# Output projections of the long sequence as seven products of halves, summed in PSUM

## The chip, the core and the metric

The kernel runs on one core of one Trainium2 chip. The metric is the device time of one execution in microseconds (us); lower is better. The core has five engines that work side by side, each with its own queue: PE (TensorE, matrix products; its weight loads, PEld, run beside them), DVE (VectorE), ACT (ScalarE), POOL (GpSimd) and SP (SyncE), which here issues nearly all DMAs. SBUF is the memory on the chip, PSUM the small memory that PE writes its sums to, DRAM the large one outside.

## The reference

Two batches share their weights: x_prompt with 512 positions (below Q, the short sequence) and x_sample with 1024 (S, the long one), 1024 channels each, in float32. There are two layers and a last norm:

```python
# even layer
p = rms_norm(x, g_norm) @ w_in                  # 1024 -> 2560
a = conv31(a_val * sigmoid(a_glu)) + conv_b     # depthwise, 512 channels
a = silu(layer_norm(a)) * silu(a_z)
f = einsum(real(fft2(f_in per group)), w_four) * silu(f_z)
x = x + concat([a, f]) @ w_out                  # 1024 -> 1024
# odd layer
u, bg, cg, z = split(rms_norm(x, g_norm) @ w_in, 4)   # 1024 -> 4096
v = conv3(cg * u) + conv_b                      # depthwise
x = x + (bg * v * silu(z)) @ w_out              # 1024 -> 1024
# at the end
y = rms_norm(x, final_norm)
```

## The kernel before, in words

Channels lie on the 128 partitions and positions along the free dimension. A tile is 128 channels x 512 positions, 8 tiles make the channels, S has two chunks of 512 positions and Q has one. A weight comes in tiles of 128 output channels with all 1024 input channels, 512 KB each.

**Precision.** A float32 matmul is done as three matmuls of a rounded type, float32r. `split` makes the high part `hi` by an ACT copy and the low part `lo = x - hi` on DVE or POOL; then high x high, high x low and low x high are added up in PSUM (`project`, L174). A projection of one tile of outputs is 3 x 8 = 24 matmuls of 512 columns. `load_w` (L133 to L135) loads and splits a weight tile, the low part on POOL.

**Products of halves.** In layer 2's input projection of S (`l2_in_two`) two tiles of output channels (128 x 2) and two chunks of positions (512 x 2) are done at once. With the input channels cut in two halves this is a 2 x 2 matrix of blocks times another, done with seven block products instead of eight (Strassen's scheme in Winograd's form). A product is 4 tiles of input channels x 3 = 12 matmuls. `halves` loads the four blocks of the left side (weights), makes the four sums s1 to s4 of them on DVE and splits the seven operands; `prep_acts_a`, `prep_acts_b` and `prep_far` make the seven right operands (activations) with their sums, two of them by way of DRAM for lack of room. `project_two` runs the seven products, each in a PSUM bank of its own (L673), and adds the results up in SBUF: one ACT copy (L677) and seven DVE adds. Both output projections (`l1_out`, and `l2_out` with `l2_out_last`) use plain projections, chunk by chunk.

**Normalization.** `SqSum` adds up squares per position over the tiles as they come (ACT square, DVE add). `rstd_bcast` sums over partitions with PE, takes the inverse root on DVE with a dozen small instructions, and spreads it with PE.

**Room.** SBUF tiles come from pools by tag with a fixed number of buffers: H 32, F 16, FQ 8, T 8, ap 4, ld 4, lx 2, dp 4. PSUM has four banks for matmul results (tag mm), two for small things (st), two for the wide convolution result (cv). What finds no room goes to DRAM and is loaded again (`ld`).

**Order.** The program text gives a priority. A planner with its own costs of instructions places each instruction on its engine's queue: it takes the ready instruction of the highest priority and may thus mix matmuls of two projections. On the chip each queue then runs in that order, whatever the real times are. The stages around the change, in the text's order: norm of Q's layer 1 result (`norm_mid`), Q's layer 2 input projection (`l2_in`, 8 steps of four projections u, c, z, b) with S's layer norms beside it, S's gates, `l1_out` of S's two chunks, operands of S (`prep_acts_a`), Q's last projection (`l2_out`) with `prep_acts_b` beside it, `prep_far`, eight steps of `l2_in_two`, `l2_out` of S's first chunk, and `l2_out_last` of its second, in two halves of 256 positions so that the end is short. `finish` scales by the last norm and stores.

## Time and profile before

| what | value |
|---|---|
| runs | 1204.4 us median of 3 (1201.76 to 1205.83) |
| profiled execution | 1203.0 us span; it has no other time of its own |
| PE busy | 1150.0 us, 96% |
| DVE, ACT, POOL busy | 77%, 36%, 32% |
| matmuls | 5328 |
| granted PE clock, mean | 0.981 of full speed |
| DMA | 145.45 MB, mean 121 GB/s |

An engine's busy time is the time in which one of its instructions runs. A matmul's row is longer than the distance to the next one's start, since they are pipelined; PE's pace is read from start to start. A group's row gives line, engine, operation, out<-in by the program's names and shapes, count, busy us, mean ns of one, and the engine's idle time before these instructions with what ended it. A timeline row gives start, duration, engine and line.

### The profile page before, as it was taken

The page shows a single profiled execution, that of the slowest core. Times are in us where ns is not written, and L with a number is a line of the kernel's source. Part 1 is how long each engine was busy: PE and PEld are TensorE (multiplying, and loading weights), DVE is VectorE, ACT ScalarE, POOL GpSimd, SP SyncE. Part 2 cuts the span into 40 slices and gives each one's busy share as a digit, 9 for nine tenths or more (in the row PEclk, how much of TensorE's full clock was granted, in tenths as well). Part 3 has the DMA queues.
Part 4 walks back from the last instruction along what each step waited for, and adds up shares of the span by engine and source line. Part 5 has one row for each costly group of instructions (what it writes and reads, how often), then busy time and mean ns, then how long its engine had stood idle before and what let it go on. Part 6 is the DMA issues. An engine that isn't in the chain of part 4 may idle for free.

```text
span 1203.0 us, 14742 instructions
## 1 busy us (share of the span) xinstructions
PE 1150.0 (96%) x5328; PEld 953.4 (79%) x5328; DVE 921.5 (77%) x1414; ACT 427.7 (36%) x673; POOL 387.6 (32%) x205
## 2 busy tenths in 40 slices
PE   7999989999998999999999998989999999999995
PEld 6777858888977887888888886778888888888894
DVE  6899999999998999854235466988877668677465
ACT  6533331224242335532224244542323233234341
POOL 3333432222234454454444433301011110103542
PEclk9999989999998999999999999999999999999997
DMA  9323212101113524232324577843212221124452
GB/s 342 105 72 122 88 36 71 53 36 53 59 65 124 185 93 141 96 123 98 122 100 171 193 262 260 287 143 128 100 54 79 90 71 68 62 96 154 149 196 88
DMA packets 64873, 145.45 MB, mean 121 GB/s; under 512 B 7200, under 2 KB 11552, under 8 KB 64800
## 3 DMA queue, kind: packets, MB, share of 16 engines
q1 hardware_dynamic: 64512, 144.21, 34.9%
q8 instruction: 42, 0.69, 0.2%
q10 hardware_dynamic: 288, 0.30, 0.1%
q14 instruction: 31, 0.25, 0.1%
HBM read 121.93 MB, written 22.54 MB: 120 GB/s over the span
## 4 chain that ended last, share of the span: by engine, by line
PE 75%; DVE 14%; DMA 3%; issue 2%; ACT 1%; SPq 0%; DVEq 0%; ACTq 0%
PE m L673 25%; PE o L174 17%; DVE cv L507 6%; PE c L174 4%; PE b L174 4%; PE z L174 4%; PE u L174 4%; PE az L174 3%; PE glu L174 3%; PE val L174 3%; PE fz L174 2%; PE fb L174 2%; PE fa L174 2%; DVE acc L110 2%; DMA y<-yd 2%
## 5 line engine op out<-in xcount | busy, mean ns | idle before, releaser
L135 POOL TENSOR_TENSOR wl<-wf,wh 128x1024 fp32r<-128x1024 f32 (+1 forms) x134 | 310.7, 2323 | 487.3 <-ACT wh L134 186.6
L134 ACT CAST wh<-wf 128x1024 fp32r<-128x1024 f32 (+1 forms) x134 | 133.1, 998 | 248.6 <-PE o L174 39.5
L507 DVE SCALAR_TENSOR_TENSOR cv<-a,par_sb,cv 128x1024 f32<-128x1024 f32 x120 | 154.2, 1285 | 1.6
L110 POOL TENSOR_TENSOR wo<-wf,wo 128x512 fp32r<-128x512 f32 x32 | 41.3, 1290 | 269.3 <-ACT wo L658 160.4
L673 PE MATMUL m<-bsh,wo 128*128 128x512 f32 x384 | 122.9, 394 | 3.9 <-ACT wo L658 3.9
L110 DVE TENSOR_TENSOR mc<-m,mc 128x512 f32<-128x512 f32 x96 | 64.6, 687 | 67.9 <-PE m L673 67.0
L110 DVE TENSOR_TENSOR acc<-acc,sq 128x512 f32<-128x512 f32 (+1 forms) x79 | 86.1, 1091 | 19.5 <-ACT sq L237 19.2
L507 DVE SCALAR_TENSOR_TENSOR cv<-ap,par_sb,cv 128x512 f32<-128x512 f32 x120 | 90.2, 752 | 2.0
L673 PEld LDWEIGHTS m<-bsh,wo 128*128 128x128 f32 x384 | 72.7, 189 | 20.2 <-ACT wo L658 4.3
L673 PE MATMUL m<-bh,wo 128*128 128x512 f32 x256 | 81.5, 390 | 0.8 <-ACT wo L658 0.8
L673 PE MATMUL m<-bfh,wo 128*128 128x512 f32 x256 | 81.6, 390 | 0.0
L673 PE MATMUL m<-bsl,wo 128*128 128x512 f32 x192 | 76.2, 397 | 0.0
L658 ACT CAST wo<-as 128x512 fp32r<-128x512 f32 x64 | 39.5, 622 | 101.6 <-PE m L673 44.2
L658 ACT CAST wo<-wf 128x512 fp32r<-128x512 f32 x48 | 29.8, 622 | 88.4 <-PE m L673 88.3
L174 PE MATMUL o<-ysh,wh 128*128 128x512 f32 (+1 forms) x256 | 56.2, 343 | 4.4 <-ACT ysh L115 4.3
L673 PEld LDWEIGHTS m<-bh,wo 128*128 128x128 f32 x256 | 48.0, 188 | 11.2 <-ACT wo L658 1.2
L174 PE MATMUL o<-yl,wh 128*128 128x512 f32 x192 | 52.1, 396 | 4.9 <-DVE yl L110 4.9
L673 PEld LDWEIGHTS m<-bfh,wo 128*128 128x128 f32 x256 | 48.1, 188 | 10.2
L174 PE MATMUL o<-ysl,wh 128*128 128x512 f32 (+1 forms) x256 | 55.5, 339 | 0.5 <-DVE ysl L110 0.5
L174 PE MATMUL o<-ysh,wl 128*128 128x512 f32 (+1 forms) x256 | 54.5, 337 | 0.0
L174 PE MATMUL o<-yh,wh 128*128 128x512 f32 x192 | 53.0, 400 | 1.2 <-ACT yh L115 1.2
L174 PE MATMUL o<-yh,wl 128*128 128x512 f32 x192 | 51.7, 392 | 0.0
(316 smaller groups left out, 2440.1 us busy)
## 6 DMA issues: line engine op xcount, KB each, us to landing
wf<-w SPq DMA_DIRECT2D x78, 512.0 KB, 3.5
wf<-w SPq DMA_DIRECT2D x68, 256.0 KB, 2.9
wf<-w1o SPq DMA_DIRECT2D x24, 512.0 KB, 3.5
wf<-w2o SPq DMA_DIRECT2D x16, 512.0 KB, 4.3
x1d<-xr SPq DMA_DIRECT2D x24, 256.0 KB, 2.1
x1r<-x1d SPq DMA_DIRECT2D x24, 256.0 KB, 3.6
y<-yd SPq DMA_DIRECT2D x22, 256.0 KB, 3.7
x<-xs SPq DMA_DIRECT2D x16, 256.0 KB, 5.4
```

Of the source, the lines that this page charges most:

```text
L110: return eng.tensor_tensor(out=out, in0=a, in1=b, op=op)
L134: nc.scalar.copy(wh[i], src_i)
L135: nc.gpsimd.tensor_tensor(out=wl[i], in0=src_i, in1=wh[i].bitcast(F32), op=ALU.subtract)
L174: nc.tensor.matmul(out[:, 0:width], a[k], act[k][b][:, cols], start=(n == 0), stop=(n == 3 * KD - 1))
L507: nc.vector.scalar_tensor_tensor(out=acc, in0=src[:, t:t + n], scalar=col(w0 + t), in1=acc, op0=ALU.mult, op1=ALU.add)
L658: nc.scalar.copy(hi, t)
L673: nc.tensor.matmul(out, w[p][a][:, k * P:(k + 1) * P], ops[p][k][b], start=(n == 0), stop=(n == 11))
```

## The change

`Pair` takes the place of `halves` and `project_two`, and now serves three projections of S: the one into layer 2 as before, and both output projections (`l1_out_two`, `l2_out_two`), in four pairs of output tiles each, for both chunks at once. The order of products is 1, 5, 2, 6, 7, 4, 3. Products 1, 6, 7 and 4 are added up in one PSUM bank (X), 5 and 3 in a second (Z), and 2 has a third (Y). Between the products of a bank its sum so far is read out: `before[..]` and `after[..]` say by what. Signs of operand 4 are changed so that it can be added. `run` makes the weights of a product three products ahead.

The right operands of the output projections are new (`out_ops`, `l2_out_ops`), and `l2_ops` takes the place of `prep_acts_a` and `prep_acts_b`. Weights come in pieces of 256 KB, four buffers of them, also in `load_w`. In the middle stage all low parts of weights are made on POOL. S's a_z and the results of layer 2 go to DRAM and back. Q's normed activations now lie in FQ and F.

The order of stages is now: norm of Q, Q's l2_in for j = 0 to 4 with S's layer norms, gates and the first operands beside them, `l1_out_two`, a second norm of Q, l2_in for j = 5 to 7 with `l2_ops` beside them, the eight steps of layer 2 of S, `l2_out_two`, and Q's output projection in half widths at the end, with S's last scaling and stores beside it.

```diff
+    def wtile():
+        return pool.tile([P, KD * P], F32R, name=nm("wo"), tag="wo", bufs=4)
...
+        t = pool.tile([P, CH], F32, name=nm("wf"), tag="wf", bufs=4)
+        nc.sync.dma_start(t, src[m, :, h * CH:(h + 1) * CH])
+        return t
...
+    def wsplit(t, hi, lo, eng):
+        nc.scalar.copy(hi, t)
+        eng.tensor_tensor(out=lo, in0=t, in1=hi.bitcast(F32), op=ALU.subtract)
...
+        for t, hi, lo in zip([wraw(src, m, h) for h in range(2)], wh, wl):
+            wsplit(t, hi, lo, nc.gpsimd)
...
-            t = pg("F" if seq is S else "FQ", "az")
+            t = pg("T" if seq is S else "FQ", "az")
+            if seq is S:
+                d = dram.tile([P, CH], F32, name=nm("azd"), tag=f"az{c}{j}", bufs=1)
+                nc.sync.dma_start(d, t)
+                t = d
...
+            az = ld("az", seq.az[c][j]) if seq is S else seq.az[c][j]
...
-        return norm_apply([ld("x1r", seq.x1[c][k]) for k in range(KD)], r, PC_N2)
+        return norm_apply([ld("x1r", seq.x1[c][k]) for k in range(KD)], r, PC_N2, (), None)
...
+    HOME = {1: "H", 5: "H", 2: "H", 6: "H", 7: "FQ", 4: "F", 3: "F"}
+    ORDER = (1, 5, 2, 6, 7, 4, 3)
+    class Pair:
...
+                a11, a21, a22, a12 = self.raw
+                s1, s2, s3, s4 = [pg("T", "as") for _ in range(4)]
+                tt(s1, a21, a22, ALU.add)
+                tt(s2, s1, a11, ALU.subtract)
+                tt(s3, a11, a21, ALU.subtract)
+                tt(s4, a12, s2, ALU.subtract)
+                self.left = {1: a11, 5: s1, 2: a12, 6: s2, 7: s3, 4: a22, 3: s4}
...
+            hl = wtile()
+            hi, lo = hl[:, 0:CH], hl[:, CH:]
+            wsplit(t, hi, lo, nc.gpsimd)
+            self.w[p] = (hi, lo)
+        def product(self, p, out, first=False):
+            n = 0
+            for some in (((0, 0), (0, 1)), ((1, 0),)):
+                for k in range(KD // 2):
+                    for a, b in some:
+                        nc.tensor.matmul(out, self.w[p][a][:, k * P:(k + 1) * P], self.ops[p][k][b],
+                                         start=(first and n == 0), stop=(n == 11), skip_group_check=True)
+                        n += 1
+        def go(self, p):
+            t, before, after = self.t, self.before, self.after
+            if p == 1:
+                self.x = ps("X")
+                self.product(1, self.x, True)
+                t[11] = before[11](self.x)
+            elif p == 5:
+                self.z = ps("Z")
+                self.product(5, self.z, True)
+                t[22] = before[22](self.z)
...
+            elif p == 2:
+                y = ps("Y")
+                self.product(2, y, True)
+                after[11](y, t[11])
+            elif p == 6:
+                self.product(6, self.x)
+                t[12] = before[12](self.x)
+            elif p == 7:
+                self.product(7, self.x)
+                after[22](self.x, t[22])
+            elif p == 4:
+                self.product(4, self.x)
+                after[21](self.x)
+            else:
+                self.product(3, self.z)
+                after[12](self.z, t[12])
...
+    def run(seq, late, look=3):
+        for i in range(-look, len(seq)):
+            if 0 <= i + look < len(seq):
+                j, p = seq[i + look]
+                j.weight(p)
+            if 0 <= i + look + 2 < len(seq):
+                seq[i + look + 2][0].load()
+            if i >= 0:
+                late.get(i, lambda: None)()
+                j, p = seq[i]
+                j.go(p)
...
+    def keep_op(ops, p, t, s, eng=nc.vector):
+        ops[p].append(split(t, HOME[p], s, eng))
...
+    def out_ops(seq, ops):
+        quad = [(seq.y1[0][4 + i], seq.y1[1][4 + i], seq.y1[0][i], seq.y1[1][i]) for i in range(4)]
+        for i, (b11, b12, b21, b22) in enumerate(quad):
+            t1, t2 = [pg("T", "bs") for _ in range(2)]
+            tt(t1, b12, b11, ALU.subtract)
+            keep_op(ops, 1, b11, "ys")
+            keep_op(ops, 5, t1, "ys", nc.gpsimd if i % 2 else nc.vector)
+            yield 1
+            keep_op(ops, 2, b21, "ys")
+            tt(t2, b22, t1, ALU.subtract)
+            keep_op(ops, 6, t2, "ys", nc.gpsimd if i % 2 else nc.vector)
+            yield 1
+        yield 0
+        for b11, b12, b21, b22 in quad:
+            t3 = pg("T", "bs")
+            tt(t3, b22, b12, ALU.subtract)
+            keep_op(ops, 7, t3, "ys")
+        yield 1
...
+        for b11, b12, b21, b22 in quad:
+            t1, t2, t4 = four()[:3]
             tt(t1, b12, b11, ALU.subtract)
             tt(t2, b22, t1, ALU.subtract)
-            tt(t3, far3, b12, ALU.subtract)
-            tt(t4, t2, b21, ALU.subtract)
-            for p, t in ((3, far3), (4, t4)):
+            tt(t4, b21, t2, ALU.subtract)
+            keep_op(ops, 4, t4, "ys")
+        yield 1
+        for i, (_, _, _, b22) in enumerate(quad):
+            keep_op(ops, 3, b22, "ys", nc.gpsimd if i % 2 else nc.vector)
+        yield 1
...
+    def l1_out_two(seq, ops):
...
+            def before(ij):
+                c, m = at[ij]
+                def run(x):
+                    t = ld("xr", seq.x[m, c])
+                    tt(t, x, t, ALU.add)
+                    return t
+                return run
...
+                def run(x, t=None):
+                    t = t if t is not None else ld("xr", seq.x[m, c])
+                    tt(t, x, t, ALU.add)
+                    sp = dram.tile([P, CH], F32, name=nm("x1d"), tag=f"x1d{seq.tag}{c}{m}", bufs=1)
+                    nc.sync.dma_start(sp, t)
+                    seq.x1[c][m] = sp
+                    acc[c].add(t)
+                return run
...
+    def l2_ops(seq, ops, far):
+        r = [rstd_bcast(seq.sm2[c].acc, D) for c in range(2)]
...
+            for c in range(2):
+                for h in range(2):
+                    x = ld("x1r", seq.x1[c][k + 4 * h])
+                    nc.vector.scalar_tensor_tensor(out=x, in0=x, scalar=col(PC_N2 + k + 4 * h), in1=r[c],
+                                                   op0=ALU.mult, op1=ALU.mult)
...
+            keep_op(ops, 1, b11, "b")
+            tt(t1, b12, b11, ALU.subtract)
+            keep_op(ops, 5, t1, "bs")
+            keep_op(ops, 2, b21, "b")
+            yield 1
+            tt(t2, b22, t1, ALU.subtract)
+            tt(t3, b22, b12, ALU.subtract)
+            tt(t4, b21, t2, ALU.subtract)
+            for p, t in ((3, b22), (7, t3), (4, t4)):
                 d = dram.tile([P, CH], F32, name=nm("bd"), tag=f"bd{p}{k}", bufs=1)
                 nc.sync.dma_start(d, t)
                 far[p].append(d)
-            for p, t, tag in ((6, t2, "H"), (7, t3, "H"), (5, t1, "FQ")):
-                ops[p].append(split(t, tag, "bs"))
-            yield
+            keep_op(ops, 6, t2, "bs")
+            yield 1
...
+        ts = [ld("bf", d) for d in far[7]]
+        yield 1
+        for p, after in ((7, 4), (4, 3), (3, None)):
+            for n, t in enumerate(ts):
+                keep_op(ops, p, t, "bf", nc.gpsimd if n % 2 else nc.vector)
+            ts = [ld("bf", d) for d in far.get(after, ())]
+            yield 1
...
+    TAKEN = {11: taken("T"), 12: taken("ap"), 22: taken("ap")}
...
+        def keep(x, t):
+            tt(t, x, t, ALU.add)
+            u[0] = t
...
+        def c0(x):
+            tp = u["tp"] = dp("tp", T + 2)
...
+            tt(tp[:, 1:1 + CH], x, u[0], ALU.mult)
+        def u1(x, t):
+            tp = u["tp"]
+            tt(t, x, t, ALU.add)
+            tt(tp[:, 1 + CH:1 + T], t, u["c1"], ALU.mult)
+            u["v"] = psum_wide()
+            taps(u["v"], tp, w0, PC_SB + j, T, 3)
...
+        def zed(c):
+            def run(x, t):
+                tt(t, x, t, ALU.add)
+                nc.scalar.activation(t, t, AF.Silu)
+                tt(t, u["v"][:, (lo, hi)[c]], t, ALU.mult)
+                u["z", c] = t
+                if c == 1:
+                    tt(u["b1"], u["b1"], t, ALU.mult)
+                    put(1, u["b1"])
+            return run
...
+        return [Pair(ops, w2, j, 16 + j, TAKEN, {11: keep, 22: c1, 21: c0, 12: u1}),
+                Pair(ops, w2, 24 + j, 8 + j, TAKEN, {11: zed(0), 22: b1, 21: b0, 12: zed(1)})]
...
+        def first(i):
+            b11, b12 = y2(0, i), y2(1, i)
+            t1 = pg("T", "bs")
+            tt(t1, b12, b11, ALU.subtract)
+            keep_op(ops, 1, b11, "ys", eng(i))
+            keep_op(ops, 5, t1, "ys", eng(i + 1))
+        def second(i):
+            keep_op(ops, 2, y2(0, i + 4), "ys", eng(i))
...
+        def sixth(i):
+            t, b11 = sums(i)
+            tt(t, t, b11, ALU.add)
+            keep_op(ops, 6, t, "ys", eng(i))
+        def rest(i):
+            b12, b22, b21 = y2(1, i), y2(1, i + 4), y2(0, i + 4)
+            t = pool.tile([P, CH], F32, name=nm("bs"), tag="ap", bufs=4)
+            tt(t, b22, b12, ALU.subtract)
+            keep_op(ops, 7, t, "ys", eng(i))
+            t = pool.tile([P, CH], F32, name=nm("bs"), tag="ap", bufs=4)
+            hi, lo = ops[6][i]
+            tt(t, b21, hi.bitcast(F32), ALU.subtract)
+            tt(t, t, lo.bitcast(F32), ALU.subtract)
+            keep_op(ops, 4, t, "ys", eng(i + 1))
+            keep_op(ops, 3, b22, "ys", eng(i))
...
+        for some in ((0, 1), (2, 3)):
+            for i in some:
+                first(i)
+            yield 1
+        for i in range(3):
+            second(i)
+        yield 1
+        for i in range(2):
+            sixth(i)
+        yield 1
+        sixth(2)
+        yield 1
+        second(3)
+        sixth(3)
+        rest(0)
+        rest(1)
+        yield 1
+        rest(2)
+        rest(3)
+        yield 1
...
+            def after(ij):
+                c, m = at[ij]
+                def run(x, t=None):
+                    t = t if t is not None else room(c, m)
+                    tt(t, x, t, ALU.add)
+                    acc[c].add(t)
+                    d = dram.tile([P, CH], F32, name=nm("x2d"), tag=f"x2d{c}{m}", bufs=1)
+                    nc.sync.dma_start(d, t)
+                    xt[c][m] = d
+                return run
...
+        def fin():
+            for c in range(2):
+                r = rstd_bcast(acc[c].acc, D)
+                for m in range(KD):
+                    o = dp("x2", 2 * CH)[:, 0:CH]
+                    nc.sync.dma_start(o, xt[c][m])
+                    nc.vector.scalar_tensor_tensor(out=o, in0=o, scalar=col(PC_N3 + m), in1=r, op0=ALU.mult, op1=ALU.mult)
+                    nc.sync.dma_start(seq.out[m, c], o)
+                    yield 1
...
             l2_out_tile(seq, c, m, w[m], act, acc[i], xt[i], ("F", "FQ")[i], int(m == 0), half[i])
+            if m > 0:
+                next(beside, None)
...
     hm = norm_mid(Q, 0)
-    for j in range(8):
-        l2_in(Q, hm, j)
-        if j < 2:
-            layer_norm(S, j)
-    gate(S, 0)
-    gate(S, 1)
-    l1_out(S, 0)
-    l1_out(S, 1)
-    ops, far, quarters = prep_acts_a(S)
-    act_q = y2_split(Q, 0)
-    fin_q = l2_out(Q, 0, act_q, prep_acts_b(S, ops, far, quarters))
-    w = halves(0, 16)
-    prep_far(ops, far)
-    for j in range(8):
-        l2_in_two(S, ops, j, w if j == 0 else None)
-        if j == 0:
-            fin_q()
-    l2_out(S, 0)()
-    l2_out_last(S, 1)
...
+    yo = {p: [] for p in range(1, 8)}
+    late = out_ops(S, yo)
+    interleave(some_l2_in(hm, range(5)), spaced(two_norms(), 2))
...
+    hm2 = []
+    seq = steps(l1_out_two(S, yo))
+    run(seq, {**on(late, 1), len(seq) - 2: lambda: hm2.extend(norm_mid(Q, 0))})
+    ops = {p: [] for p in range(1, 8)}
+    far = {3: [], 7: [], 4: []}
+    interleave(some_l2_in(hm2, range(5, 8)), l2_ops(S, ops, far))
+    zo = {p: [] for p in range(1, 8)}
+    jobs_out, fin_s = l2_out_two(S, zo)
+    two = steps([x for j in range(KD) for x in l2_two(S, ops, j)])
+    seq = two + steps(jobs_out)
+    act_q = []
+    run(seq, {**on(prep_far(ops, far)), **on(l2_out_ops(S, zo), len(two) - 5), **on(y2_split(Q, 0, "H", act_q), len(seq) - 6)})
+    l2_out_last(Q, 0, act_q, fin_s())
```

More of the change, by code (lines that the diff above doesn't have):

```diff
@@ new lines, in steps, with four @@
+    def steps(jobs):
+        return [(j, p) for j in jobs for p in ORDER]
+    def run(seq, late, look=3):
[9 more added lines that the diff above has]
+                j.go(p)
+    def four():
+        return [pool.tile([P, CH], F32, name=nm("bs"), tag="ap", bufs=4) for _ in range(4)]
@@ L663, in project_two @@
-    def project_two(ops, w, c11, c12, c21, c22):
-        wd = c11.shape[-1]
-        def product(p):
-            out = ps("m")[:, 0:wd]
-            n = 0
-            for pairs in (((0, 0), (0, 1)), ((1, 0),)):
-                for k in range(KD // 2):
-                    for a, b in pairs:
-                        nc.tensor.matmul(out, w[p][a][:, k * P:(k + 1) * P], ops[p][k][b], start=(n == 0), stop=(n == 11))
-                        n += 1
-            return out
-        nc.scalar.copy(c12, product(1))
-        tt(c11, product(2), c12, ALU.add)
-        tt(c12, product(6), c12, ALU.add)
-        tt(c21, product(7), c12, ALU.add)
-        p5 = product(5)
-        tt(c12, p5, c12, ALU.add)
-        tt(c22, p5, c21, ALU.add)
-        tt(c12, product(3), c12, ALU.add)
-        tt(c21, c21, product(4), ALU.subtract)
@@ L723, in l2_out_tile @@
         pq = project("o2", w, act, order, cols)[:, 0:wd]
[L724 to L729 removed]
+        x2 = pg(tag, "x2")[:, 0:wd]
         tt(x2, pq, xr, ALU.add)
```

260 lines of the change are left out of this document (133 added, 127 removed).

## The prediction

> **What bounds the kernel now.** I read the page first, then the busy times by stretch, then the chain of waits in order of time, then groups by shape, and last the timeline at two places.
>
> ```profile
> span 1203.0 us, 14742 instructions
> PE 1150.0 (96%) x5328; PEld 953.4 (79%) x5328; DVE 921.5 (77%) x1414; ACT 427.7 (36%) x673; POOL 387.6 (32%) x205
> ```
>
> PE is busy 96% of the span, so a change counts by what it does to PE's work or to PE's few holes. The holes show in the stretches; an x behind an engine is its instructions.
>
> ```profile
> core 0: us, PE busy (x) PEld busy (x) DVE busy (x) ACT busy (x) POOL busy (x), PEclk, DMA share, GB/s
> 457.00:480.00 23.00, 21.33 (x85) 16.85 (x85) 20.97 (x31) 13.86 (x21) 9.16 (x5) 0.93 0.45 152
> 480.00:690.00 210.00, 210.00 (x939) 174.09 (x938) 104.62 (x145) 70.78 (x94) 96.74 (x41) 1.00 0.37 129
> 720.00:750.00 30.00, 25.21 (x102) 18.64 (x100) 20.11 (x41) 14.57 (x24) 9.23 (x5) 0.94 0.77 256
> 750.00:780.00 30.00, 30.00 (x133) 24.59 (x131) 29.04 (x37) 13.91 (x21) 10.73 (x5) 1.00 0.85 286
> 780.00:810.00 30.00, 25.37 (x107) 20.42 (x107) 26.98 (x54) 13.62 (x25) 3.89 (x3) 0.94 0.51 163
> 810.00:1100.00 290.00, 290.00 (x1274) 238.87 (x1273) 219.87 (x344) 89.73 (x150) 42.21 (x31) 1.00 0.25 85
> 1140.00:1188.00 48.00, 46.77 (x390) 46.48 (x388) 27.25 (x73) 20.27 (x45) 16.85 (x14) 1.00 0.45 150
> ...
> 573.11 5.44 PE u L174 x24
> ```
>
> From 480 to 690 and from 810 to 1100 PE has no hole. The last row, from the chain, prices a 512-column matmul: 5.44/24 = 0.2267 us from start to start, 4.41 a us, 132.3 in 30 us, and 2.72 us for a product of twelve. By that, 720 to 750 lacks 30 and 780 to 810 lacks 25: (30.3 + 25.3) x 0.2267 = 12.6 us lost where the long sequence's layer 2 operands are made. The chain in those 70 us:
>
> ```profile
> 711.15 4.11 DMA x1r<-x1d
> 717.28 3.96 DMA hd<-x1r
> 722.18 5.81 DMA y<-yd
> 786.42 2.78 DMA bf<-bd
> ```
>
> It runs through loads, not through PE.
>
> **The change, part by part.** *Matmuls.* Each output projection of the long sequence has 2 chunks x 8 tiles x 24 = 384 matmuls of 512 columns (layer 2's second chunk as twice as many halves). As 4 pairs x 7 products x 12 it has 336. Two projections: 96 x 0.2267 = **-21.8**. PE is the engine that sets the end there, so this counts whole. The half-width products stay, for the short sequence, at the end.
>
> *The cover of the operand stage.* `l2_ops` now runs beside three l2_in tiles of the short sequence, 12 x 5.44 = 65 us of PE, where `prep_acts_b` had eight output tiles, 43.5 us. Its own DVE work, 4 x (4 scalings of 0.74, 4 sums and 4 differences), is 44 us at the prices below, which fits beside the l2_in tiles' few. I take all of the loss back: **-12.6** (bounds 0 and -12.6). The layer norms, gates and operands 1, 5, 2 and 6 of `out_ops` go beside the first five l2_in tiles, 20 x 5.44 = 109 us of PE in a stretch where DVE was busy 105 of 210: 0. Without that cover the 20 instructions of `out_ops` alone would be 20 us.
>
> *DVE and POOL in the middle stage.*
>
> ```profile
> L110 DVE TENSOR_TENSOR mc<-m,mc 128x512 f32<-128x512 f32 x96 | 64.6, 687 | 67.9 <-PE m L673 67.0
> L110 DVE TENSOR_TENSOR mc<-mc,m 128x512 f32<-128x512 f32 x16 | 10.9, 683 | 2.0 <-PE m L673 2.0
> L110 DVE TENSOR_TENSOR wo<-as,wo 128x512 fp32r<-128x512 f32 x64 | 43.5, 686 | 0.1
> L110 POOL TENSOR_TENSOR wo<-wf,wo 128x512 fp32r<-128x512 f32 x32 | 41.3, 1290 | 269.3 <-ACT wo L658 160.4 <-DVE mc L110 106.6 <-issue 2.3
> L677 ACT COPY mc<-m 128x512 f32<-128x512 f32 x16 | 9.3, 581 | 0.0
> L110 DVE TENSOR_TENSOR acc<-acc,sq 128x512 f32<-128x512 f32 x65 | 79.1, 1217 | 14.6 <-ACT sq L237 14.3
> L110 DVE TENSOR_TENSOR bsl<-bs,bsh 128x512 fp32r<-128x512 f32 x12 | 12.0, 1025 | 0.0
> L135 POOL TENSOR_TENSOR wl<-wf,wh 128x1024 fp32r<-128x1024 f32 x118 | 290.1, 2460 | 466.7 <-ACT wh L134 178.9 <-PE o L174 47.0 <-PE az L174 43.6
> ```
>
> Seven adds a pair on DVE become three, 16 x 4 x 0.687 = 44 us less; two more copies on ACT, 32 x 0.581 = 19 us more; five low parts a pair go from DVE to POOL, 55 us off DVE and 80 x 1.29 = 103 on. POOL then has 145 of 290 us, a pair's seven 9.0 us of its 19. All of it at **0**: PE hides it, having no hole from 810 to 1100 with DVE at 220. Without that cover POOL would be the next bound, and it is at half. Ordinary weights in two halves cost POOL at most 2 x 1.29 - 2.46 = 0.12 us a tile: 0 too.
>
> Those rows carry a second price. `mc<-m,mc` reads PSUM and takes 0.687 us; the same shape from SBUF alone takes 1.025 and 1.217 in stages where POOL works. So I price the new SBUF sums and differences at 1.0. The Trainium skill, "SBUF — State Buffer", Who interferes with whom, says why: a DVE instruction with two SBUF inputs contends with a GpSimd one that reads SBUF. These rows agree; by a price of 0.687 instead, start (a) below would cost 0, and the sum would be 3 less.
>
> *The chains' waits.* Products 1, 6, 7 and 4 add up in one bank. Before 7 may write, 6's sum must be copied out (ACT in layer 2, a DVE add in the output pairs); before 4 may, DVE must have read 7's. Behind the waiting matmul on PE stand 7, 4 and all after them, and for these wait the next pair's results. Rows for such a step:
>
> ```profile
> 907.70 1.07 PE L673 MATMUL m<-bh,wo 128*128 128x512 f32 x4
> 908.87 0.69 DVE L110 TENSOR_TENSOR mc<-m,mc 128x512 f32<-128x512 f32 x1 [1.39 <-PE m L673]
> ...
> 1194.46 0.48 DVE L218 TENSOR_SCALAR dh<-cst_sb,yh 128x128 fp32r<-128x128 f32 x2
> 1195.08 0.55 PE L222 MATMUL r<-dh,ones_r 128*128 128x256 f32 x1 [6.39 <-DVE dh L218]
> ```
>
> The last of a product's matmuls starts 3 x 0.2267 after 907.70, at 908.38, so PE could go on at 908.61; it ends at 908.77, and DVE begins 0.10 later. From DVE's end (1194.94) to PE's start is 0.14. An empty wait costs 0.16 + 0.10 + 0.69 + 0.14 = 1.09 us with DVE, 0.98 with ACT. Layer 2: 16 pairs x 2.07; the outputs: 8 x 2.18; in all 50.6 us for 48 waits. That is the upper bound; the lower is 0, if the planner puts matmuls of product 3 (another bank, its weights three products ahead) or of the next pair into the gap: product 3 is 2.72 us of work, and a pair's two gaps are 2.1 to 2.2. What it did with a like gap:
>
> ```profile
> 113.37 0.61 PE L418 MATMUL z<-wcs,eo 128*128 128x128 f32 x4
> 113.73 1.39 PE L174 MATMUL az<-rl,wh 128*128 128x512 f32 x5
> 114.06 0.37 ACT L421 CAST zh<-z 128x256 fp32r<-128x256 f32 x1 [1.52 <-PE z L418]
> 114.47 0.42 DVE L110 TENSOR_TENSOR zl<-z,zh 128x256 fp32r<-128x256 f32 x1
> 114.96 1.99 PE L174 MATMUL az<-rh,wl 128*128 128x512 f32 x8
> 116.78 0.28 PE L449 MATMUL pq<-tbh,zh 128*128 128x256 f32 x1
> ```
>
> While ACT and DVE worked on z, PE did thirteen matmuls of a projection and then pq, with no hole. So I take a tenth of the bound: **+5**.
>
> *The starts.* Four times PE needs operands that cannot be made long before, since buffers come free only then. (a) The first pair of `l1_out_two`: products 7, 4 and 3 take tiles that the last l2_in frees. DVE owes 4 x 2 for 7, 4 x 4 for 4 and 2 for 3, 26 instructions or 26 us at 1.0, with some 5 of the pair's own; PE has 4 to 6 products, 11 to 16 us, and two of the next pair, 5.4. What DVE did ahead is unknown: +3. (b) The short sequence is normed a second time, eight loads and sixteen DVE instructions, when products 7, 4 and 3 of the last pair free its tiles. The first norming is in the trace: 457 to 480 lacks 101.5 - 85 = 16.5 matmuls, **+3.7**. (c) The first layer 2 pair, twelve far operands from DRAM: +2. (d) The first pair of `l2_out_two`, 32 loads of y2 of 256 KB through four tiles; at 4 us a load and hold, 32 us against some nine products, 25: +4. For a, c and d the nearest row is 720 to 750: each 0 to 30.3 x 0.2267 = 6.9. Sum **+12.7**.
>
> *The end.* S's results go by way of DRAM and are scaled beside the last stage: 16 loads and 16 stores more, 8.4 MB, and 16 x 0.74 on DVE.
>
> ```profile
> L746 DVE SCALAR_TENSOR_TENSOR x<-x,par_sb,r 128x512 f32<-128x512 f32 x16 | 10.7, 738 | 0.9 <-PE r L223 0.9
> GB/s 342 105 72 122 88 36 71 53 36 53 59 65 124 185 93 141 96 123 98 122 100 171 193 262 260 287 143 128 100 54 79 90 71 68 62 96 154 149 196 88
> ```
>
> From 1140 to 1188 DVE has 27 of 48 us, and DMA moves 150 GB/s; with 8.4/48 us = 175 more it is 325, under the 342 of the first slice, but near. SP's queue carries them among the last weights, in order, and a store waits there for DVE: **+1** (0 to 8). The other new transfers (a_z and y2 of S by DRAM) lie under full PE: 0.
>
> *Sum:* 1203.0 - 21.8 - 12.6 + 5 + 12.7 + 1 = 1187.3. The runs' median, 1204.4, is 1.4 above the profiled span, the only figure given of that execution: **1189**.
>
> **The rivals.** *Clean* (0.14): the planner hides waits and starts, as at 480 and 810, where stages change without a hole: 1203.0 - 34.4 + 1.4 = 1170. Against it: (b) has no more cover than two products. *Starts as dear as before* (0.10): three starts at 6.9 and the cover of `l2_ops` too short by what 780 to 810 lost, 5.7: 1189 + 11.7 + 5.7 = 1206, no change. For it: DVE was at 29 of 30 us from 750 to 780 and POOL now works more. *Chains not filled* (0.14), the other side: the planner's times for ACT and DVE are short of the chip's, or product 3's weights come late from POOL, and each wait stands open: 1189 + 45.6 = **1235**. It decides from 5 + 15.4 = 20.4 us over 48 waits, 0.42 us each, on. For it: POOL is new in the path of every product; against it, the timeline at 113. The Trainium skill, "Perfetto Trace Analysis", Matmuls, speaks for this rival: independent matmul groups should rotate through PSUM banks so that one's evacuation overlaps the next's matmuls. The change gives that up for four products of seven; no run here shows such a chain yet.
>
> **How the numbers follow.** The forecast has 0.62. A measurement of this kernel tells 0.3%, 3.6 us, from no change. Forecast and clean case are faster: 0.76; dear starts are the same: 0.10; open chains slower: 0.14. The range leaves the open chains out and goes from just under the clean case to just past the dear starts, 1167 to 1209; the forecast's own is 1174 to 1202.
>
> **What would show it.** Matmuls: 96 fewer of 512 columns. The chains: product 3 split around 7 in the timeline, and PE waits for ACT or DVE under 10 us in all over the two-chunk products; over 20 and I am wrong. The starts: holes of 2 to 4 us at four places, none over 7. DVE's share falls in the middle stage with PE still full. The DMA share stays under 0.95 in the last 50 us. If the time falls under 1170, the waits and starts cost nothing.

## The result, and the profile after

The changed kernel takes 1254.4 us (median; three runs from 1251.7 to 1255.1, and one of 4024.8, far out of line, which doesn't enter the ratio), the kernel before on the same chip 1204.7. The ratio is 1.040, 95% interval 1.038 to 1.043: **slower by 50 us**, where 1189 and a range up to 1209 were forecast. The case that the prediction gave for a slower kernel, open chain waits, isn't what came true: the middle stage, where most of the chains are, loses nothing.

The page of the kernel after, its span and busy times:

```profile
span 1252.0 us, 15335 instructions
PE 1151.2 (92%) x5242; PEld 942.8 (75%) x5242; DVE 952.9 (76%) x1406; ACT 464.7 (37%) x847; POOL 565.8 (45%) x421
```

The matmuls are gone as announced: 96 of 512 columns fewer, and ten more for the second norm of Q (two of 512 columns, eight narrow), so 86 less. PE's share still fell from 96% to 92%. POOL went from 388 to 566 us. The busy times by stretch show where PE stands:

```profile
core 0: us, PE busy (x) PEld busy (x) DVE busy (x) ACT busy (x) POOL busy (x), PEclk, DMA share, GB/s
540.00:600.00 60.00, 47.09 (x190) 36.64 (x190) 49.88 (x60) 20.95 (x38) 31.32 (x21) 0.91 0.24 78
660.00:690.00 30.00, 23.12 (x84) 16.70 (x83) 18.96 (x34) 7.64 (x13) 7.54 (x6) 0.77 0.51 159
720.00:780.00 60.00, 46.77 (x176) 35.80 (x175) 51.08 (x58) 23.80 (x43) 31.57 (x21) 0.86 0.61 197
780.00:1050.00 270.00, 270.00 (x1186) 222.34 (x1185) 139.85 (x171) 89.12 (x156) 132.12 (x99) 1.00 0.24 78
1050.00:1110.00 60.00, 36.60 (x136) 27.41 (x135) 52.01 (x59) 24.57 (x43) 35.33 (x23) 0.79 0.59 184
1200.00:1252.00 52.00, 32.74 (x248) 31.58 (x246) 35.03 (x92) 11.47 (x28) 11.84 (x14) 0.84 0.66 213
```

A full 60 us hold 265 matmuls of 512 columns. The first row has 190: (265 - 190) x 0.2267 = 17 us lost. 1050 to 1110 lost 29. From 780 to 1050, the stage with the chained products, nothing is lost.

To compare all kernels of this case I add up, over all matmuls of a trace, the distance to the next matmul's start as far as it is above the pace (0.2267 us for 512 columns, 0.12 for 256; 0.06 is taken for narrower ones), sorted by the time at which it stands. The columns are named by what the kernel after does at that time. Experiments are single runs, but for e6, e13 and e15 with 4 to 8; the kernel before, run beside them, took 1204.7 to 1206.9. In us:

| kernel | time | to 540 | first pair of layer 1's output, 540-630 | second norm, 630-720 | first pair of layer 2, 720-810 | products of layer 2, 810-1020 | first pair of the last projection, 1020-1140 | end |
|---|---|---|---|---|---|---|---|---|
| before | 1204.7 | 54.6 | 0.2 | 0.8 | 16.6 | 1.6 | 1.1 | 9.4 |
| after | 1254.4 | 45.2 | 18.9 | 16.5 | 20.7 | 1.5 | 31.6 | 19.3 |
| e1, POOL only writes | 1209.1 | 43.4 | 6.8 | 15.7 | 6.3 | 1.5 | 20.3 | 14.9 |
| e2, low parts on DVE | 1233.3 | 45.6 | 12.3 | 16.1 | 9.4 | 1.5 | 28.1 | 19.7 |
| e3, layer 2's output plain | 1226.6 | 44.8 | 19.7 | 15.6 | 20.0 | 1.6 | 3.7 | 10.6 |
| e4, layer 1's output plain | 1231.0 | 48.2 | 1.4 | 3.7 | 13.9 | 1.7 | 32.1 | 19.5 |
| e5, both plain | 1203.8 | 48.2 | 1.4 | 3.4 | 13.8 | 1.7 | 4.2 | 10.2 |
| e6, both plain, low parts on DVE | 1197.5 | 45.4 | 1.3 | 3.6 | 9.2 | 1.5 | 6.2 | 8.9 |
| e7, e1 without reloads | 1193.1 | 41.2 | 6.3 | 9.6 | 7.4 | 1.5 | 7.0 | 19.4 |
| e8, before, low parts on POOL | 1203.8 | 57.5 | 0.2 | 0.8 | 13.4 | 1.5 | 0.6 | 9.4 |
| e9, after without reloads | 1241.6 | 41.2 | 19.0 | 7.2 | 16.6 | 1.6 | 27.2 | 28.3 |
| e10, e2 with layer 2's output plain | 1211.0 | 44.7 | 13.4 | 17.6 | 8.1 | 1.5 | 4.5 | 10.5 |
| e11, e2 with layer 1's output plain | 1216.8 | 45.3 | 1.3 | 3.5 | 9.3 | 1.5 | 28.4 | 16.9 |
| e12, e2 without reloads | 1214.1 | 41.2 | 11.4 | 11.0 | 8.2 | 1.5 | 18.5 | 21.8 |
| e13, e6 with two far operands | 1194.9 | 45.6 | 1.3 | 2.1 | 6.1 | 1.5 | 6.3 | 8.8 |
| e14, e6 with all on DVE | 1194.0 | 51.2 | 1.4 | 2.0 | 1.4 | 1.5 | 7.1 | 8.9 |
| e15, e13 and e14 | 1192.8 | 49.2 | 1.4 | 2.0 | 0.7 | 1.5 | 6.0 | 8.8 |

After less before: -9.4 + 18.7 + 15.7 + 4.1 - 0.1 + 30.5 + 9.9 = +69.4, and -21.8 for the matmuls: 47.6 of the 49.0 us between the two spans.

**The chains.** The timeline around a chain in the middle stage, X being the bank of products 1, 6, 7 and 4:

```profile
906.88 1.07 PE L641 MATMUL X<-bsh,wo 128*128 128x512 f32 x4
907.79 0.39 PE L641 MATMUL Z<-bfh,wo 128*128 128x512 f32 x1
908.72 0.57 ACT L797 COPY mc<-X 128x512 f32<-128x512 f32 x1
909.60 1.07 PE L641 MATMUL Z<-bfh,wo 128*128 128x512 f32 x4
910.51 0.40 PE L641 MATMUL X<-bfh,wo 128*128 128x512 f32 x1
```

Product 6 ends, ACT copies its sum, and meanwhile PE does the twelve matmuls of a product 3 in bank Z; product 7 starts at 910.51 with no wait. From 780 to 1050 PE waits for nothing. Its waits for the reader of bank X, over the whole trace:

```profile
PE X L641 <- DVE x L110: 10.4, 2, 9.3
PE X L641 <- DVE xr L110: 9.6, 1, 9.6
PE X L641 <- ACT mc L797: 4.8, 2, 3.8
```

That is 24.8 us, of which 23.7 stand at first pairs: 9.6 at 585 (layer 1's output), 4.8 between 720 and 780 (layer 2), 9.3 at 1100 (layer 2's output).

**The first pair of layer 1's output.** DVE's, PE's and POOL's timelines:

```profile
575.53 1.48 DVE L110 TENSOR_TENSOR bs<-a,bs 128x512 f32<-128x512 f32 x1
576.93 1.74 DVE L110 TENSOR_TENSOR as<-wf,as 128x512 f32<-128x512 f32 x1
578.60 2.48 DVE L110 TENSOR_TENSOR bs<-a,fh 128x512 f32<-128x512 f32 x4
581.00 1.75 DVE L110 TENSOR_TENSOR bs<-a,bs 128x512 f32<-128x512 f32 x1
582.68 1.75 DVE L110 TENSOR_TENSOR bs<-fh,fl 128x512 f32<-128x512 f32 x1
584.35 0.68 DVE L110 TENSOR_TENSOR xr<-X,xr 128x512 f32<-128x512 f32 x1
...
585.18 0.76 PE L641 MATMUL X<-ysh,wo 128*128 128x512 f32 x1 [9.59 <-DVE xr L110]
585.74 0.63 PE L641 MATMUL X<-ysl,wo 128*128 128x512 f32 x1
586.17 0.63 PE L641 MATMUL X<-ysh,wo 128*128 128x512 f32 x1
...
575.19 2.94 POOL L130 TENSOR_TENSOR wo<-as,wo 128x512 fp32r<-128x512 f32 x2 [2.54 <-ACT wo L129]
580.53 1.68 POOL L130 TENSOR_TENSOR wo<-wf,wo 128x512 fp32r<-128x512 f32 x1 [2.40 <-DVE bs L110]
582.17 1.71 POOL L130 TENSOR_TENSOR wo<-as,wo 128x512 fp32r<-128x512 f32 x1
```

A chain does wait here, but not for its own 1.09 us: the add that frees bank X (584.35) stands in DVE's queue behind operands for later products, and DVE is without a gap. The same kind of instruction takes 0.68 us or 1.75: the long ones lie beside POOL's low parts, and in POOL's gap from 578.13 to 580.53 four are done in 2.48 us. No run changes the order of DVE's queue, so what that order costs by itself isn't shown. And the hole costs more than its length: after it the matmuls start 0.43 us apart, not 0.2267; the granted clock from 570 to 600 was 0.83.

**What makes DVE slow.** Groups by shape in the middle stage, 810 to 1050, first before, then after:

```profile
L110 DVE TENSOR_TENSOR tp<-mc,mc 128x512 f32<-128x512 f32 x14 | 9.5, 686 | 0.0
L110 DVE TENSOR_TENSOR as<-wf,as 128x512 f32<-128x512 f32 x12 | 8.2, 681 | 0.0
```

```profile
L110 DVE TENSOR_TENSOR tp<-mc,mc 128x512 f32<-128x512 f32 x7 | 12.7, 1812 | 0.2
L110 DVE TENSOR_TENSOR mc<-X,mc 128x512 f32<-128x512 f32 x19 | 13.1, 690 | 17.6 <-PE X L641 17.6
L130 POOL TENSOR_TENSOR wo<-as,wo 128x512 fp32r<-128x512 f32 x50 | 66.4, 1329 | 77.0 <-ACT wo L129 77.0
```

The instruction with both inputs in SBUF went from 686 to 1812 ns; the one that reads a PSUM bank stayed at 690. Over the whole trace of after, the DVE sums, differences and products of 512 columns with both inputs in SBUF take 1.196 us where a POOL sum or difference runs beside them (215 of them) and 0.684 where none does (232); those that read PSUM take 0.687 and 0.686. That is 215 x 0.51 = 110 us of DVE's time. In the middle stage it is hidden; at the starts DVE is what PE waits for. The Trainium skill, "SBUF — State Buffer", Who interferes with whom, says that a DVE instruction with two SBUF inputs contends with a GpSimd instruction that reads SBUF, and that one with at most one SBUF input, outside the two-port modes, doesn't. The rows agree with that; the section gives no duration for this pair.

**The second norm** is a chain of loads, and **the first pair of the last projection** one of loads and slow DVE work. The chain of waits at 660 and 1050, and PE's waits there:

```profile
658.34 4.55 DMA x1r<-x1d
662.98 0.75 DVE x1r L241
663.73 1.44 DVE nl L110
665.19 2.62 DMA x1r<-x1d
667.91 0.75 DVE x1r L241
...
by line: DMA y<-yd 34.3%; DVE bs L110 19.5%; DVE as L110 15.4%; issue 12.7%; DVE ysl L110 10.5%; DVE mc L110 3.4%; DVE cv L510 2.4%; ACT wo L129 1.2%; SPq L1034 1.1%; ACT mc L797 0.9%; DVE tp L110 0.6%; DVEq L110 0.3%
```

```profile
PE u L173 <- ACT nh L115: 6.8, 4, 2.6
...
PE X L641 <- DVE x L110: 9.3, 1, 9.3
PE Y L641 <- ACT ysh L115: 8.8, 1, 8.8
```

In the second norm each of four loading tiles is loaded, scaled and split before the next load into it starts, and PE waits for the copies `nh`. At the last projection's start a third of the chain is loads of y2, and most of the rest DVE's; of PE's two long waits there one is for an operand, one for the add that frees bank X.

### The profile page after: what moved, and what is told of

It is laid out like the page before. It is cut to its first block, busy times and chain, and to the rows that moved or that the text cites. A ratio compares the mean times of both kernels' runs of the same rounds, so it can differ in the third digit from the quotient of the medians.

```text
span 1252.0 us, 15335 instructions
## 1 busy us (share of the span) xinstructions
PE 1151.2 (92%) x5242; PEld 942.8 (75%) x5242; DVE 952.9 (76%) x1406; ACT 464.7 (37%) x847; POOL 565.8 (45%) x421
## 4 chain that ended last, share of the span: by engine, by line
PE 31%; DVE 11%; DMA 7%; issue 3%; ACT 1%; POOL 0%; SPq 0%; DVEq 0%; ACTq 0%
PE X L641 16%; PE Z L641 7%; PE Y L641 4%; DVE as L110 2%; DVE bs L110 2%; DMA x1r<-x1d 2%; DMA y<-yd 2%; PE o L173 1%; DVE ysl L110 1%; PE u L173 1%; PE b L173 1%; DMA x<-x2d 1%; DVE x L110 1%; DMA wf<-w2o 1%; DVE acc L110 0%
## 5 line engine op out<-in xcount | busy, mean ns | idle before, releaser
L130 POOL TENSOR_TENSOR wo<-wf,wo 128x512 fp32r<-128x512 f32 x246 | 337.8, 1389 | 459.7 <-ACT wo L129 324.9
L129 ACT CAST wo<-wf 128x512 fp32r<-128x512 f32 x248 | 145.6, 619 | 228.8 <-PE X L641 57.2
L130 POOL TENSOR_TENSOR wo<-as,wo 128x512 fp32r<-128x512 f32 x96 | 133.0, 1387 | 127.4 <-ACT wo L129 126.8
L641 PE MATMUL X<-ysh,wo 128*128 128x512 f32 x256 | 88.8, 412 | 24.4 <-DVE x L110 10.4
L641 PE MATMUL X<-bfh,wo 128*128 128x512 f32 x256 | 87.0, 401 | 1.1 <-ACT mc L797 1.0
L641 PEld LDWEIGHTS X<-ysh,wo 128*128 128x128 f32 x256 | 50.7, 198 | 39.7 <-DVE x L110 11.5
L641 PEld LDWEIGHTS X<-bfh,wo 128*128 128x128 f32 x256 | 49.2, 192 | 13.4 <-ACT mc L797 2.0
L641 PE MATMUL X<-ysl,wo 128*128 128x512 f32 x128 | 52.8, 412 | 0.0
L641 PE MATMUL X<-bfl,wo 128*128 128x512 f32 x128 | 51.2, 400 | 0.0
L110 DVE TENSOR_TENSOR as<-wf,as 128x512 f32<-128x512 f32 x24 | 21.8, 909 | 30.2 <-DMA wf<-w 19.2
L641 PE MATMUL Z<-bsh,wo 128*128 128x512 f32 x128 | 44.3, 389 | 0.0
```

Source lines behind the costliest of these rows:

```text
L110: return eng.tensor_tensor(out=out, in0=a, in1=b, op=op)
L129: nc.scalar.copy(hi, t)
L130: eng.tensor_tensor(out=lo, in0=t, in1=hi.bitcast(F32), op=ALU.subtract)
L641: nc.tensor.matmul(out, self.w[p][a][:, k * P:(k + 1) * P], self.ops[p][k][b], start=(first and n == 0), stop=(n == 11), skip_group_check= ...
```

## The experiments

Three theories of the lost 49 us. *Port*: DVE is slowed by POOL's new reads. *Load*: the operands come back from DRAM through four tiles. *Work*: DVE has too much to do in the starts, slowed or not.

**e1: POOL writes only.** From Q's first norm on, each of POOL's low parts is zeroed instead of computed.

```diff
-            wsplit(t, hi, lo, nc.gpsimd)
+            nc.scalar.copy(hi, t)
+            nc.gpsimd.memset(lo.bitcast(F32), 0.0)
```

> From the second layer on POOL writes a zero low part instead of subtracting (left out: the low parts that POOL makes from there on), so it reads nothing while DVE works. Port theory (DVE's SBUF operations wait for POOL, the adds that a chain needs stand behind them in DVE's queue): DVE operations of 512 columns over 0.9 us all but vanish, the holes at the first output pair of layer 1, the first pair of layer 2 and the first output pair of layer 2 shrink by about the 13, 17 and 16 us that DVE lost to slow operations there: 1205 to 1220. Load theory (reloads from DRAM through four tiles set the pace of the operands): the holes stay, 1243 to 1255.

Measured 1209.1: 45 us back. From 441 us on, 108 of DVE's 475 sums, differences and products of 512 columns take over 0.9 us in the kernel after, and one in e1. DVE in the first pair's stretch does more instructions in less time than after (60 instructions in 49.88 us):

```profile
540.00:600.00 60.00, 56.82 (x245) 45.27 (x243) 40.57 (x75) 25.75 (x45) 12.74 (x25) 1.00 0.33 106
```

The loss at that pair falls from 18.9 to 6.8, at layer 2's from 20.7 to 6.3, at the last projection's from 31.6 to 20.3; the second norm's stays. Port holds for the first two. But zeroing also shortens POOL's work (its memset takes 0.5 us, not 1.3 to 1.7), so e1 alone doesn't part the port from POOL's own lateness.

**e2: the low parts on DVE.** Nothing left out; paired weights and operands:

```diff
-            wsplit(t, hi, lo, nc.gpsimd)
+            wsplit(t, hi, lo, nc.vector)
...
-        ops[p].append(split(t, HOME[p], s, eng))
+        ops[p].append(split(t, HOME[p], s))
```

> All low parts of paired weights and of operands on DVE, none on POOL; nothing is left out. Port theory: a POOL operation that meets a DVE operation costs DVE about 1.1 us, the same work on DVE 0.6, so the starts lose less: 1225 to 1240. Load theory: same holes, 1250 to 1258. Work theory (DVE simply has too much to do while PE's cover lasts): more work on DVE at the starts, slower, 1258 to 1275.

Measured 1233.3: **giving DVE more work made the kernel 21 us faster**. With POOL silent from 810 to 1050, `tp<-mc,mc` is back at 686 ns:

```profile
L110 DVE TENSOR_TENSOR tp<-mc,mc 128x512 f32<-128x512 f32 x6 | 4.1, 686 | 0.0
```

**e3, e4, e5: the plain projections again**, e3 layer 2's, e4 layer 1's (with it the second norm goes), e5 both, with everything else as after. `l2_out_plain` makes each tile by `project` and sends it to DRAM for the same `fin` as after.

```diff
-    jobs_out, fin_s = l2_out_two(S, zo)
+    main_s, fin_s = l2_out_plain(S)
...
-    run(seq, {**on(late, 1), len(seq) - 2: lambda: hm2.extend(norm_mid(Q, 0))})
+    l1_out(S, 0)
+    l1_out(S, 1)
+    hm2 = hm
```

> Only the layer 2 output projection of the long sequence undone: plain projections, two chunks one after the other, results by way of DRAM and the end as in the changed kernel. 48 more matmuls cost 10.9 us. Start theory (the 29.6 us that PE lacks from 1050 to 1110 belong to making the seven operands): 1235. If the hole only moves to the plain projection's own operands or to the end: 1254 to 1265.

> Only the layer 1 output projection of the long sequence undone: plain projections, no second norm of the short sequence. 48 more matmuls cost 10.9 us. Start theory: the holes at the first output pair (14.8 us) and at the second norm (12.8 us) go: 1237. If they only move behind: 1254 to 1265.

> Both output projections are plain again (96 matmuls of 512 columns more than the changed kernel), the second norm of Q is gone, the seven products of layer 2 with their chained banks and POOL's low parts stay. If the starts alone made the loss, the two single undoings add up: 1254 - 27.7 - 23.4 = 1203 us (1197 to 1210), the first pair of layer 2 still loses about 20 us between 720 and 780, and no hole over 3 us stands elsewhere between 480 and 1100. If the chains or POOL's part in the middle stage cost anything of themselves, it stays above 1215.

Measured 1226.6, 1231.0 and 1203.8. e3 and e4 gain 8 and 6 us more than expected; the end, which falls by 8.7 in e3, and the first pair of layer 2, by 6.8 in e4, weren't counted. Each projection costs 23 to 28 us more than it saves in matmuls, and the two add up (1254.4 - 27.8 - 23.4 = 1203.2). So the seven chained products of layer 2 alone, with POOL's low parts, make no loss: e5 is level with the kernel before.

**e8: the low parts of before on POOL.**

```diff
-            tt(lo, t, hi.bitcast(F32), ALU.subtract, nc.gpsimd if p in (1, 4) else nc.vector)
+            tt(lo, t, hi.bitcast(F32), ALU.subtract, nc.gpsimd)
```

> The kernel before with one edit: all seven low parts of a pair's weights on POOL, not two, in the middle stage, where PE has no hole. Port theory: DVE's sums of weight halves (SBUF alone) rise from 0.68 to 0.85 us or more and POOL's low parts from 1.29 to 1.4, DVE's adds that read PSUM stay at 0.69; PE covers it, so the time stays within 4 us of the kernel before. Rival (POOL's slowness is a property of the changed kernel's tiles): both durations stay as they were. If the time rises by 10 us or more, POOL in the products' path costs even under a full PE.

Measured 1203.8, no change; groups and busy times from 810 to 1050 (for the groups to 1100):

```profile
L110 DVE TENSOR_TENSOR as<-wf,as 128x512 f32<-128x512 f32 x15 | 22.3, 1489 | 0.0
L110 POOL TENSOR_TENSOR wo<-as,wo 128x512 fp32r<-128x512 f32 x60 | 80.0, 1336 | 85.4 <-ACT wo L658 84.2 <-DVE ysl L110 1.1
```

```profile
810.00:1050.00 240.00, 240.00 (x1055) 197.78 (x1054) 165.63 (x221) 69.01 (x114) 117.80 (x90) 1.00 0.25 84
```

The same row of before:

```profile
810.00:1050.00 240.00, 240.00 (x1055) 197.67 (x1054) 180.95 (x287) 70.05 (x118) 33.28 (x26) 1.00 0.23 81
```

So the slowing isn't a property of the changed kernel's tiles: with the old ones, too, the sum `as<-wf,as` goes from 681 ns (the row of before above) to 1489. And this prices the move by itself: 66 instructions off DVE, at 0.687 worth 45 us, took only 15 off its busy time and put 84.5 on POOL. Under a full PE that shows in no time.

**e7, e9, e12: no reloads.** A constant tile stands in for the loaded y2 and, in the second norm, for the loaded and scaled x1.

```diff
-            return seq.y2[c][k] if k == KD - 1 else ld("y2", seq.y2[c][k])
+            return seq.y2[c][k] if k == KD - 1 else flat
...
-lambda: hm2.extend(norm_mid(Q, 0))
+lambda: hm2.extend(split(flat, ("FQ", "F")[k // 4], "n") for k in range(KD))
```

e7 has it with e1's silent POOL, e9 with the kernel after as it is, e12 with e2's low parts on DVE.

> The run with POOL writing zeros, and besides the loads of y2 for the last projection's operands and the second norm's loads, sums and scalings left out: a constant tile stands in for both. Its starts lost 19 us (1020 to 1080) and 11 us (630 to 660) with the loads in. Load theory (the rest of the loss is loads through four tiles): both fall under 4 us, 1209 - 24 = 1185 us (1180 to 1190). Buffer theory (the operands' places come free only when the products before have ended, and the copies and low parts alone then take longer than the two or three products of cover): both stay over 7 us, 1200 us or more.

> The changed kernel with all its low parts on POOL, and only the loads of y2 for the last projection's operands and the second norm's loads, sums and scalings left out (a constant tile stands in). With POOL writing zeros the same cut took 13.3 us from the last projection's start and 6.1 from the second norm's. Separate causes: it takes the same here, 1254 - 19 = 1235 us (1229 to 1239), and the start of the last projection still loses about 18 us. Joint cause (DVE only falls behind because loads come late and bunch its work; with the loads gone it has time enough even beside POOL): that start loses under 9 us, 1254 - 23 - 7 = 1224 us or less.

> Both projections as seven products, all low parts of paired weights and operands on DVE, and the y2 loads and the second norm's loads, sums and scalings left out. It tells what the change could give if its operands had room in SBUF. Separate causes: 1233 - 13 - 6 = 1214 us (1208 to 1220). Loads as the carrier of the whole rest: the starts of the last projection and the second norm fall under 9 us each, 1233 - 21 - 8 = 1204 us or less. Under 1195 only if the first pair of layer 1's output projection (12 us) falls with them.

Measured 1193.1, 1241.6 and 1214.1. e12's time is what separate causes give. e7 lies between its two theories: 7.0 and 9.6 us stay at its two places, not under 4, and the end loses 4.5 more than in e1. e9 misses both expectations. At the last projection's start the loss is 31.6 with both, 27.2 without the loads, 20.3 without POOL's reads, and 7.0 without either: what is taken away singly shows less than its share, since the other bound is right behind. DVE's busy time from 1030 to 1070, in e9, e12 and then e7, shows why:

```profile
1030.00:1070.00 40.00, 31.67 (x131) 25.34 (x129) 39.93 (x41) 16.89 (x31) 28.67 (x17) 0.91 0.15 48
```

```profile
1030.00:1070.00 40.00, 31.27 (x122) 23.36 (x120) 40.00 (x64) 14.84 (x26) 0.00 (x0) 0.87 0.23 73
```

```profile
1030.00:1070.00 40.00, 38.47 (x166) 30.75 (x166) 29.88 (x50) 19.03 (x35) 10.77 (x22) 1.00 0.35 112
```

DVE never rests in e9 and e12. Beside POOL it gets 41 instructions done, alone 64, and even these are too many: 18.5 us are still lost in e12, where DVE also makes the low parts that the kernel after gives to POOL. In e7 POOL writes zeros for them, DVE has room, and 7.0 are lost. So loads and POOL's low parts together hold 24.6 of this start's 31.6 us; where DVE takes the low parts over, its work costs 11.5 of them again. e7 doesn't part DVE's slowing from the time that POOL itself takes. With e12 at 1214 the change wouldn't pay with room for its operands either, unless some of DVE's work went too.

**e10, e11: one projection as seven products, on e2's ground.** e10 is e2 with e3's edit, e11 e2 with e4's.

> Only layer 1's output projection of S keeps the seven products, layer 2's is plain, and all low parts of paired weights and operands are on DVE. From the run with both (1233.3): the last projection's start is gone (28.1 to 3.7 us lost), the end falls by 9, 48 matmuls come back (10.9): 1211 us (1205 to 1217). What is left over the kernel before is the first pair of that projection, 12, and the second norm, 16. Rival: the single projection is worth its 48 matmuls, under 1195.

> Only layer 2's output projection of S keeps the seven products; layer 1's is plain, with no second norm; all low parts of paired weights and operands on DVE. From the run with both (1233.3): 11 us at the first pair and 12.5 at the second norm are saved, 10.9 of matmuls come back: 1221 us (1214 to 1228), with 28 us lost between 1020 and 1140. Rival: under 1195, if the two projections disturb each other.

Measured 1211.0 and 1216.8, as expected. With both plain (e6, below) it is 1197.5, so neither is worth its 48 matmuls.

**e6, e13, e14, e15: what is left to win.** e6 is e5 with e2's edit: layer 2's chained products, plain output projections, low parts on DVE.

> As the run with both projections plain, and the low parts of the paired weights and of the operands on DVE. Port theory (DVE's instructions are slow while POOL reads SBUF): the first layer 2 pair's loss falls from 20 to about 9 us, so 1191 us (1184 to 1198), faster than the kernel before by 1%. Work theory (DVE has too much to do): the middle stage takes 112 low parts of 0.69 us = 55 us more on DVE, at 220 of 290 us before, minus 44 us of adds that the chains save; were that too much, holes of over 5 us would open between 810 and 1100 and the time would stay at 1203 or more.

Measured 1197.5, ratio to the kernel before 0.993 (0.991 to 0.996). Faster, by less than 1% and less than expected: the first layer 2 pair's loss ends at 9.2, as the port theory had it, but comes down from e5's 13.8, not from 20. Two edits go after that rest. e13 makes the operand of product 7 at once, and in e14 the plain weights' low parts, too, go to DVE from Q's sixth step on:

```diff
# e13
-    HOME = {1: "H", 5: "H", 2: "H", 6: "H", 7: "FQ", 4: "F", 3: "F"}
+    HOME = {1: "H", 5: "H", 2: "H", 6: "H", 7: "F", 4: "FQ", 3: "F"}
...
-            for p, t in ((3, b22), (7, t3), (4, t4)):
+            for p, t in ((3, b22), (4, t4)):
...
+            keep_op(ops, 7, t3, "bs")
# e14
-            wsplit(t, hi, lo, nc.gpsimd)
+            wsplit(t, hi, lo, nc.vector if late_w else nc.gpsimd)
```

> As the run with both projections plain and the low parts on DVE (1197.5 us, 9.2 us lost between 720 and 810), and the operand of product 7 made at once in the free half of F: two operands of the first layer 2 pair come back from DRAM, not three, and eight transfers go. Load theory (that pair waits for far operands through the four loading tiles): the loss there falls under 5 us, 1193 us (1189 to 1196). Work theory (DVE is behind since the stage before, where it has no idle time): it stays at 8 us or more, 1197 us (1195 to 1200).

> As the run with both projections plain and the low parts on DVE, and from the short sequence's sixth step of layer 2 on the plain weights' low parts on DVE too, so that POOL reads nothing there. Port theory (7.5 us of slow DVE instructions between 690 and 720 make the first pair late): the loss between 720 and 810 falls from 9.2 to under 5 us, 1193 us. Work theory (24 low parts of 0.69 us, 16 us, are put on a DVE that idles 0.1 of 30 us there): the loss stays at 8 us or more, 1197 to 1205 us, and more holes open in the last stage.

e13: 1194.9, ratio 0.992 (0.989 to 0.995), 6.1 us lost, between its two theories. e14: 1194.0 in one run, and the loss is all but gone, 1.4, as the port theory had it. From 690 to 750 e6, then e14:

```profile
690.00:720.00 30.00, 28.99 (x124) 22.94 (x123) 29.86 (x38) 10.93 (x20) 15.45 (x10) 1.00 0.80 264
720.00:750.00 30.00, 25.85 (x95) 20.16 (x94) 21.09 (x35) 13.02 (x24) 0.00 (x0) 0.83 0.48 148
```

```profile
690.00:720.00 30.00, 30.00 (x131) 24.33 (x130) 29.76 (x51) 13.75 (x25) 0.00 (x0) 1.00 0.77 251
720.00:750.00 30.00, 29.55 (x129) 23.96 (x129) 25.80 (x44) 15.23 (x28) 0.00 (x0) 1.00 0.66 201
```

DVE is full in both, with 38 instructions beside POOL and 51 alone. The hole (PE lacks 37 matmuls between 720 and 750) comes after the slow instructions, when POOL is already silent. But the chain of waits in e6 from 690 to 750 has POOL's own low parts on 16.1%, with 3.45 us of them (714.83) right before a weight's load, and far operands' loads on 15.0%. So e14 shows that POOL's low parts make this hole, but not how much of it comes by way of DVE and how much by POOL's own time. e14 loses 5.8 us more before 540, where its program text is e6's; why is open.

> The last two together: both output projections plain, all low parts from the short sequence's sixth step of layer 2 on DVE, product 7's operand without its way through DRAM. If the loss at the first layer 2 pair was one loss with one cause (POOL's reads, 9.2 to 1.4 us), the way through DRAM adds nothing to that cure, and the time is that of the better one alone, 1193 us (1190 to 1197), against 1205 for the kernel before. If they were two losses, up to 3 us less, 1190 us.

e15: **1192.8 us, ratio to the kernel before 0.988 (0.986 to 0.990)**, the best version; the two theories are 3 us apart, which e14's single run can't tell, but by place the loss only goes from 1.4 to 0.7, so the second cure finds next to nothing left. The row for the first layer 2 pair:

```profile
720.00:780.00 60.00, 60.00 (x265) 49.41 (x264) 48.24 (x78) 25.44 (x45) 0.00 (x0) 1.00 0.36 119
```

## Why the prediction was wrong, point by point

**Matmuls, -21.8: right.** 96 fewer of 512 columns, at the same pace.

**Chains, +5: nothing under way, 23.7 us at the first pairs.** The stretch from 780 to 1050, with some 14 of layer 2's 16 pairs, lost nothing. By the prediction's own sign, waits for ACT or DVE over 20 us, its account of the waits is wrong all the same: 24.8 us for the reader of X alone. They aren't 48 small waits, as the rival of open waits had it, but a few long ones, where the start's operands hold up the add that frees the bank. The sum priced waits and starts as two terms that don't touch; these are one loss, and in the table it is counted under the starts. So that rival had the right sign and the wrong place. The bank rule of the Trainium skill, "Perfetto Trace Analysis", Matmuls, that spoke for it isn't hurt: the planner rotates among X, Z and Y across pairs, and by the timeline at 906 a copy lies under another bank's product.

**The starts, +12.7: this is the step that failed.** By place they cost 18.7 (a), 15.7 (b), and 30.5 (d); (c) can't be parted from the operand stage. The bound of 6.9 for a, c and d, taken from the dearest such stretch of before, held nowhere. Three things were wrong in it. The first is the term for (a): "26 us at 1.0 ... What DVE did ahead is unknown: +3". By its own figures 31 us of DVE stand against 16 to 21 of PE and lack 10 to 15 (at 0.687, still 1.5 to 6.5, not the 0 that it states); the +3 was a guess at what is unknown. And the price of 1.0 lies between two that the chip has, 0.68 and 1.75; beside POOL's low parts it is the second. In e1, where POOL reads nothing, (a) still loses 6.8, so about 12 of its 18.9 are the port and POOL's own pace; the rest isn't parted. The second is that (d) counted loads alone, "32 us against some nine products", and not DVE's 38 instructions of operands beside the pairs' own work, nor POOL beside them: leaving the loads out (e9) gives 4.4 of 31.6 us, leaving out POOL's low parts as well (e7) 24.6. The third is that a hole of 9 us was priced at its length, while the clock (0.58 of full speed from 1080 to 1110, in that stretch) makes it longer. For (b), leaving out its loads, sums and scalings takes 5.1 to 9.3 of some 16 us; 7.2 to 11.0 stay, and what makes them is open. The row taken, 457 to 480, had half of its loads landed by 418.

**POOL's part, "All of it at 0: PE hides it": right for the middle stage, wrong as a whole.** e8 and the stretch 780 to 1050 bear out the cover. But the same edit runs in the starts, where there is none, and there it cost 21 us net (after against e2). Once DVE's slower prices beside POOL were read, the question to ask was where POOL reads while DVE is what PE waits for; the working used them for (a) and the operand stage alone.

**The operand stage, -12.6: not got.** "44 us at the prices below, which fits": from 720 to 810 the loss rose from 16.6 to 20.7. Without the seven products of layer 1's output before it the stage loses 13.9 (e4). e14 shows that the cover can suffice (1.4) when both outputs are plain and POOL is silent; for the kernel as changed that isn't shown.

**The end, +1 (0 to 8): dearer.** 9.9 by place. e3 has 10.6 there against 19.3, so it comes with S's layer 2 output in pairs; which of its transfers or sums does it is open.

**Not forecast:** 9.4 us less lost before 540; the other kernels with the new text lose 41 to 51 there. Weights in halves are the new thing in that stretch, but no run tests them alone.

## What to carry to other kernels

Price a step that is moved to another engine by both engines' rows *while both work*: here (e8) a low part moved from DVE to POOL freed 0.23 us of DVE (15.3 / 66), not 0.69, and cost POOL 1.3. At a change of stages, where the next operands and the current results share one queue in a planned order, look for what stands ahead of the instruction that frees a bank. When two causes lie behind one hole, taking each away alone shows little: take both away in one run before calling either small.
